# The turn between two transformer layers: an order by hand, weights of the last MLP group split once, first unit's three token tiles in open banks, tables kept in DRAM

## The chip, the cores and the metric

The kernel runs on one core of one Trainium2 chip. The metric is the device time of one launch in microseconds (us), the median of several executions. TensorE is called PE below, VectorE DVE, ScalarE ACT, GpSimd POOL; SP is the engine whose queue issues every DMA of this kernel, strictly in order.

## What is computed

The reference runs two layers over 128 prompt tokens and 512 latent tokens of width 1024, all float32. Cut to what matters here:

```python
def _layer(x, mod, p, lam_init, ctx_kv, rope):
    sh1, sc1, g1, sh2, sc2, g2 = jnp.split(mod, 6, axis=-1)
    h = _rmsnorm(x, p['norm1']) * (1 + sc1) + sh1
    qa, ka, va, qb, kb, vb, uc = jnp.split(h @ p['w_in'], splits, axis=-1)
    qa = _rmsnorm(qa.reshape(b, s, 2, A_HEADS, A_DH), p['qn_a'])      # ka, qb, kb alike
    if rope is not None:
        qa = _apply_rope(qa, cos, sin)                                 # ka, qb, kb alike
    ...
    oa = _diff_attention(qa, ka, va, lam)
    ob = _gqa_attention(qb, kb, vb)
    oc = _pool_mixer(uc, p['w_pool'], p['pool_scale'])
    merged = ga * (oa @ p['w_br_a']) + gb * (ob @ p['w_br_b']) + gc * (oc @ p['w_br_c'])
    x = x + g1 * (merged @ p['w_out'])
    h2 = _rmsnorm(x, p['norm2']) * (1 + sc2) + sh2
    a, g = jnp.split(_dwconv3(h2 @ p['w_up'], p['conv_w'], p['conv_b']), 2, axis=-1)
    x = x + g2 * ((jax.nn.silu(a) * g) @ p['w_down'])
    return x, own_kv
```

Layer 1 starts with the norm of the x that layer 0's last line gives, so nothing of layer 1 can start before x is whole in a token. That turn is the place of the change.

## The kernel before

All 640 tokens stay in SBUF, features on partitions: x is eight blocks of 128 features by 640 tokens. Every matrix product is three matmuls in a rounded 32-bit format (mm3, lines 111 to 114): an operand is split into a high part, written by ACT (line 95), and the rest, written by DVE (line 96). A weight goes through load_w (lines 98 to 106): a DMA into st (three buffers), ACT writes wh, DVE writes wl (five buffers each). A weight is therefore usable one transfer, one ACT instruction and one DVE instruction after its issue.

**The end of a layer.** The MLP's 22 feature blocks are taken in four groups (GROUPS). For the last, blocks 17 to 21, the down projection is made per token chunk, CH_A = (0 to 384), (384 to 640), with a product of five blocks for each of eight outputs n, and the weight of an output is loaded and split again in each chunk: 16 loads of 640 columns (lines 1029 to 1047). After each output DVE adds the product to x (down_add, line 881), ACT squares it, POOL sums the squares over n (DVE the last), and SP stores x to x_dram (line 1043). At the end of a chunk rms1_chunk (line 231) makes the norm: ones times the sum on PE (stat), DVE's ms, POOL's power (rr), one diagonal matrix dg for each 128 tokens on DVE, and ones times dg on PE, which spreads the factor over the partitions (bc). Then modulate (lines 200 to 210) makes the next layer's input: for each feature block k DVE writes ht, ACT the high part hh, DVE the low part hl, in pieces of 128 and 256 tokens.

**The start of a layer.** attention_phase (line 238) first makes the tables of the rotation (cg, sg: lines 247 to 277) on DVE from cos, sin and a few rows of parameters, and the number nlam. Then it works through six units of the input projection. A unit (line 303) has four weights of 768 columns and five token tiles of 128; a tile is eight products of 384 columns in one PSUM bank (mm), which ACT empties into raw (line 361), then squares (366) and sums (368), the rotation (379 to 389) and the transposes (tr) follow. The units are woven with attention tasks of the unit before and with other items ("u" the mixer's input, "g" the gates, "p" the pooling's projection), by the table FILL.

**What sets the order.** No instruction order is written out: the framework's scheduler takes the program and chooses, by a model of its own and the data each instruction needs, the order in which each engine gets it. On the chip each engine works through its list strictly in order, and an instruction that waits holds all behind it.

Of the kernel before, what the change touches and what calls it, by code (L numbers as in the profile page):

```python
# [12 lines left out]
F32 = mybir.dt.float32  # L13
F32R = mybir.dt.float32r
AF = mybir.ActivationFunctionType
ALU = mybir.AluOpType
# [40 lines left out]
def trunk_kernel(ctx: ExitStack, tc: tile.TileContext, a: dict):  # L57
# [34 lines left out]
    x_dram = dram.tile([P, ND, T], F32, name="x_dram")  # L92

# [144 lines left out]
    def attention_phase(l, hh, hl, w0):  # L238
        lam_init = 0.8 - 0.6 * math.exp(-0.3 * l)
        with ExitStack() as st:  # L240
# [5 lines left out]
            rows = ap.tile([P, 8, 64], F32, tag="dup", name="rowv")  # L246
            dma(rows, a["rowv"][l])

            lt = ap.tile([P, 2, 64], F32, tag="sq", name="lt", bufs=4)
            lam2 = small.tile([P, 2], F32, tag="lam2", name="lam2", bufs=1)  # L250
            nlam = small.tile([P, 1], F32, tag="nlam", name="nlam", bufs=1)
            vec.tensor_tensor(out=lt[:, 0], in0=rows[:, 4], in1=rows[:, 5], op=ALU.mult)
            vec.tensor_tensor(out=lt[:, 1], in0=rows[:, 6], in1=rows[:, 7], op=ALU.mult)
            vec.tensor_reduce(out=lam2, in_=lt, axis=AX.X, op=ALU.add)
            act.activation(lam2, lam2, AF.Exp)
            vec.tensor_tensor(out=nlam, in0=lam2[:, 1:2], in1=lam2[:, 0:1], op=ALU.subtract)
            vec.tensor_scalar_add(out=nlam, in0=nlam, scalar1=-lam_init)

            vec.tensor_scalar_mul(out=rows[:, 0:4:2], in0=rows[:, 0:4:2], scalar1=0.125)
            cos = late.tile([P, 4, 64], F32, tag="w", name="cos", bufs=4)  # L260
            sin = late.tile([P, 4, 64], F32, tag="w", name="sin", bufs=4)
            dma(cos, a["cos"])
            dma(sin, a["sin"])
            cgs, sgs = [], []
            for kind in range(2):
                cg = ap.tile([P, 5, 2, 64], F32, tag=f"cg{kind}", name=f"cg{kind}", bufs=1)
                sg = ap.tile([P, 4, 2, 64], F32, tag=f"sg{kind}", name=f"sg{kind}", bufs=1)
                for typ in range(2):
                    g = rows[:, 2 * kind + typ:2 * kind + typ + 1]
                    vec.tensor_copy(cg[:, 0:1, typ], g)  # L270
                    vec.tensor_tensor(out=cg[:, 1:, typ], in0=cos, in1=g.to_broadcast([P, 4, 64]), op=ALU.mult)
                    for h in range(2):
                        hs, ho = slice(32 * h, 32 * h + 32), slice(32 - 32 * h, 64 - 32 * h)
                        vec.tensor_tensor(out=sg[:, :, typ, hs], in0=sin[:, :, hs],
                                          in1=g[:, :, ho].to_broadcast([P, 4, 32]), op=ALU.mult)
                cgs.append(cg)
                sgs.append(sg)
# [25 lines left out]
            def unit(kind, idx, w, out, prefetch):  # L303
# [41 lines left out]
                late_tr = None  # L345
                out.extend((qk, v1, v2))
                for tt in range(5):
                    ts = slice(tt * P, (tt + 1) * P)
                    ps = ps_m.tile([P, 384], F32, tag="mm", name="mm")
                    for k in range(ND):  # L350
                        hi, lo = w[k // 2]
                        ws = slice((k % 2) * 384, (k % 2) * 384 + 384)
                        mm3(ps, hh[:, k, ts], hl[:, k, ts], hi[:, ws], lo[:, ws], k == 0, k == 7)
                        yield 0.49
                    if late_tr is not None:
                        transposes(*late_tr)
                        yield 0.5
# [41 lines left out]
                    late_tr = (dup.rearrange("p h a d -> p h (a d)"), nh, nq, qk, slot)  # L399
                transposes(*late_tr)  # L400
                yield 0.5

# [296 lines left out]
            for i, items in enumerate(FILL):  # L699
                stream.extend([("unit", i)] * (i < len(order)) + items)  # L700
# [16 lines left out]
            def run(i, made=None):  # L717

                kind, n = stream[i]
                w = loaded[i]  # L720
                if kind == "unit":
                    yield from unit(*order[n], w, made, lambda: prefetch(i + 1))
# [9 lines left out]
            for i, items in enumerate(FILL):  # L732
                made = []
                n = len(items)
                if i < len(order):
                    n += 1
                own = chain.from_iterable(run(j, made) for j in range(at, at + n))
# [146 lines left out]


# [85 lines left out]
    sst.close()  # L971
    for l in range(L):
        dst.close()
        xst.close()
        attention_phase(l, hh, hl, w0)
        w0 = None
# [16 lines left out]
        with ExitStack() as ms:  # L993
# [11 lines left out]
            for gi, (f0, f1) in enumerate(GROUPS):  # L1005
# [17 lines left out]
                if l + 1 < L:  # L1023
                    hst = ExitStack()
                    hp = tp("h1p", 1, hst, side="right")
                    hh = hp.tile([P, ND, T], F32R, name="hh")
                    hl = hp.tile([P, ND, T], F32R, name="hl")
                    A1 = scale_cols(l + 1, V_N1, 8, "A1")
                for c, (a0, b0) in enumerate(CH_A):
                    acc = Acc(rp, b0 - a0)  # L1030
                    for n0 in range(0, 8, 2):
                        ps = ps_d.tile("dl")
                        for j in range(2):
                            n = n0 + j
                            hi, lo = load_w(a["w_down"][l, n, :, f0 * P:f1 * P], nf * P)
                            for i in range(nf):
                                ks = slice(i * P, (i + 1) * P)
                                mm3(ps[:, j, :b0 - a0], hi[:, ks], lo[:, ks], fs[i][0][:, a0:b0],
                                    fs[i][1][:, a0:b0], i == 0, i == nf - 1)
                            down_add(l, x, n, ps[:, j], a0, b0)  # L1040
                            if l + 1 < L:
                                acc.add(x[:, n, a0:b0], n == 7)
                                dma(x_dram[:, n, a0:b0], x[:, n, a0:b0])
                            else:
                                dma(a["y"][:, n, a0:b0], x[:, n, a0:b0])
                    if l + 1 < L:
                        rms1_chunk(l + 1, c, rp, x, hh, hl, ps_d, acc, A1)
# [114 lines left out]
```

## Time and profile before

| | |
|---|---|
| median of three runs | 2300.72 us (2298.7 to 2303.47) |
| the profiled execution's own time | 2307.55 us |
| its span in the profile | 2305.3 us |
| mean granted PE clock | 0.988 of full speed |
| busy share of the span: PE, DVE, ACT, POOL | 97%, 68%, 42%, 23% |
| DMA, mean over the span | 112 GB/s |

The profile is one execution. PE's matmuls are pipelined, so their listed durations overlap: the distance from one start to the next is what a matmul costs, and a busy PE can still run at half clock. The shares are means over stages with different limits: what holds between the layers has to be read from the windows there, 1135 to 1230 us.

### The profile page before, as it was taken

To read this page: it belongs to the slowest core of one execution; us is meant where nothing else is said; L and a number is where in the kernel's file an instruction comes from. 1 tells how busy PE (TensorE), PEld (TensorE's weight loads), DVE (VectorE), ACT (ScalarE), POOL (GpSimd) and SP (SyncE) were. 2 spreads that over 40 slices of the span, in tenths; PEclk is the share of its full clock that TensorE was granted. 3 is DMA by queue.
4 is the path that set the end of the run, shared out by engine and by line. 5 is a ranking of instruction groups with operands and counts; after the bars stand their busy time and mean duration, and the time that the engine had idled before them with its cause. 6 is when DMAs were issued, how large, how long until landed. Compare 5 with 4: busy or idle time off the path is not lost. (4 is left out here: it accounts for less than half of the span.)

```text
span 2305.3 us, 37922 instructions
## 1 busy us (share of the span) xinstructions
PE 2225.9 (97%) x14778; PEld 2163.6 (94%) x14778; DVE 1562.8 (68%) x2913; ACT 975.7 (42%) x1728; POOL 528.4 (23%) x651
## 2 busy tenths in 40 slices
PE   8898999999999999999979999999999999999999
PEld 4898989989999999999969989899999999999999
DVE  6877687559567756765587867864895676554555
ACT  4555555432244423333355645653323453242422
POOL 3753443024041000000047533320422200000000
PEclk8999999999999999999999999999999999999999
DMA  7211223367333333432242112224762332322123
GB/s 256 80 57 59 82 66 107 108 244 228 121 121 106 101 104 121 135 102 88 75 128 83 57 49 83 97 89 135 283 210 89 123 110 92 94 65 90 50 84 114
DMA packets 102775, 258.50 MB, mean 112 GB/s; under 512 B 19523, under 2 KB 32579, under 8 KB 102596
## 3 DMA queue, kind: packets, MB, share of 16 engines
q1 hardware_dynamic: 102596, 256.09, 34.1%
q8 instruction: 116, 1.90, 0.3%
q14 instruction: 63, 0.51, 0.1%
HBM read 233.10 MB, written 22.95 MB: 111 GB/s over the span
## 5 line engine op out<-in xcount | busy, mean ns | idle before, releaser
L95 ACT ACTIVATE wh<-st 128x1024 fp32r<-128x1024 f32 (+3 forms) x336 | 314.7, 943 | 297.0 <-PE dn L114 170.8
L113 PE MATMUL up<-h2l,wh 128*128 128x320 f32 x1408 | 435.6, 310 | 2.5 <-DVE h2l L209 2.4
L112 PE MATMUL up<-h2h,wl 128*128 128x320 f32 x1408 | 433.5, 310 | 2.4 <-ACT v L862 1.4
L114 PE MATMUL up<-h2h,wh 128*128 128x320 f32 x1408 | 435.0, 310 | 0.0
L96 DVE TENSOR_TENSOR wl<-st,wh 128x1024 fp32r<-128x1024 f32 (+3 forms) x336 | 375.4, 1120 | 71.7 <-ACT wh L95 71.1
L113 PEld LDWEIGHTS up<-h2l,wh 128*128 128x128 f32 x1408 | 265.2, 189 | 3.6 <-DVE h2l L209 3.6
L112 PEld LDWEIGHTS up<-h2h,wl 128*128 128x128 f32 x1408 | 264.5, 189 | 4.0 <-ACT h2h L208 2.1
L114 PEld LDWEIGHTS up<-h2h,wh 128*128 128x128 f32 x1408 | 265.3, 189 | 0.1
L143 DVE SCALAR_TENSOR_TENSOR junk<-stm,cs 128x1024 bf16<-128x1024 f32 x172 | 223.2, 1298 | 60.1 <-DMA stm<-in_w_mod 57.2
L865 DVE SCALAR_TENSOR_TENSOR v<-u,vecs,v 128x127 f32<-128x127 f32 (+1 forms) x176 | 89.1, 547 | 183.4 <-ACT v L862 183.4
L112 PE MATMUL mm<-wh,hl 128*128 128x384 f32 x480 | 169.5, 353 | 15.0 <-ACT raw L361 10.8
L113 PE MATMUL dn<-al,wh 128*128 128x320 f32 x544 | 168.1, 309 | 0.0
L114 PE MATMUL dn<-ah,wh 128*128 128x320 f32 x544 | 168.1, 309 | 0.0
L112 PE MATMUL dn<-ah,wl 128*128 128x320 f32 x544 | 168.1, 309 | 0.0
L113 PE MATMUL mm<-wl,hh 128*128 128x384 f32 x480 | 163.7, 341 | 2.6 <-DVE wl L96 2.6
L114 PE MATMUL mm<-wh,hh 128*128 128x384 f32 x480 | 163.4, 340 | 0.0
L114 PE MATMUL gp<-hh,wh 128*128 128x320 f32 x480 | 148.6, 310 | 0.0
L112 PE MATMUL gp<-hh,wl 128*128 128x320 f32 x480 | 148.4, 310 | 0.0
L113 PE MATMUL gp<-hl,wh 128*128 128x320 f32 x480 | 148.3, 309 | 0.0
L112 PE MATMUL mmu<-hh,wl 128*128 128x384 f32 (+1 forms) x416 | 134.0, 322 | 4.0 <-ACT up L677 2.0
L114 PE MATMUL mmu<-hh,wh 128*128 128x384 f32 (+1 forms) x416 | 131.0, 315 | 0.0
L113 PE MATMUL mmu<-hl,wh 128*128 128x384 f32 (+1 forms) x416 | 130.4, 314 | 0.0
(226 smaller groups left out, 5444.6 us busy)
## 6 DMA issues: line engine op xcount, KB each, us to landing
stm<-in_w_mod SPq DMA_DIRECT2D x88, 512.0 KB, 4.3
st<-in_w_up SPq DMA_DIRECT2D x88, 512.0 KB, 3.6
st<-in_w_gate SPq DMA_DIRECT2D x48, 512.0 KB, 4.4
st<-in_w_unit SPq DMA_DIRECT2D x48, 384.0 KB, 3.2
st<-in_w_out SPq DMA_DIRECT2D x32, 512.0 KB, 3.6
st<-in_w_down SPq DMA_DIRECT2D x48, 320.0 KB, 3.0
st<-in_w_br SPq DMA_DIRECT2D x24, 512.0 KB, 3.6
st<-in_w_down SPq DMA_DIRECT2D x32, 384.0 KB, 3.2
```

The costliest lines, as they stand in the source:

```text
L95: act.activation(hi, x, AF.Copy)
L96: eng.tensor_tensor(out=lo, in0=x, in1=hi.bitcast(F32), op=ALU.subtract)
L112: pe.matmul(out, sl, mh, start=start, stop=False)
L113: pe.matmul(out, sh, ml, start=False, stop=False)
L114: pe.matmul(out, sh, mh, start=False, stop=stop)
L143: vec.scalar_tensor_tensor(out=junk, in0=st, scalar=1.0, in1=cs[:, j], op0=ALU.mult, op1=ALU.mult, accum_out=col)
L865: vec.scalar_tensor_tensor(out=v[:, s + 1:e], in0=u[:, s:e - 1], scalar=cw[0], in1=v[:, s + 1:e], op0=ALU.mult, op1=ALU.add)
```

## The change

Between layer 0 and layer 1 a new function, turn_over, takes the place of the loop over the two chunks. All of it stands in a block in which every engine keeps the order of the source.

- The weights of the last group are loaded as five tiles of 1024 columns and split once; both chunks use them. They fill all five wh and wl buffers for as long as both chunks run.
- The square of output 0 is written into the sum directly. One diagonal instruction for a whole chunk takes the place of one for each 128 tokens.
- The four weights of layer 1's first unit are loaded within chunk 1, one after the products of each of the outputs 4 to 7.
- The first three token tiles of the first unit are summed in the banks ps_a and ps_b, opened by turn_over. PE's order in that unit is the source's too, and one "u" item moves into it.
- The rotation tables of layer 1 are computed at the end of layer 0's attention (prepare_next), stored to tab_dram and read back by four DMAs in layer 1.

The diff, cut to its core:

```diff
+            def prepare_next():
+                rows = late.tile([P, T], F32, tag="w", name="rowv", bufs=4)...
+                dma(rows, a["rowv"][1])
+                cs2 = rotation()
...
+                for kind, cg, sg in prepare(1, rows, cs2, into):
+                    dma(tab_dram[2 * kind], wide[f"cg{kind}"])
+                    dma(tab_dram[2 * kind + 1][:, :512], wide[f"sg{kind}"][:, :512])
...
+            fill = [FILL[1][:1], FILL[1][1:]] + FILL[2:] if ahead else FILL
...
+                if i == 0 and ahead:
+                    with tc.manual_schedule(engines={mybir.EngineType.PE}):
+                        for _ in run(0, made):
+                            pass
...
+            if l + 1 < L:
+                prepare_next()
             for _ in chain(flush(), *(run(j) for j in range(at, len(stream)))):
...
+    def turn_over(l, x, rp, fs, f0, hh, hl, ps_d, A):
...
+        load(0)
+        load(1)
+        tile_of = lambda c, n: ps_d.pools[(4 * c + n // 2 + 1) % 3].tile([P, 2, 512], F32, tag="d", name="dl")
+        for n in range(8):
+            if n % 2 == 0:
+                ps = tile_of(0, n)
+            products(0, n, ps)
+            if n in (0, 2, 4):
+                load(2 + n // 2)
+            evac(0, n, ps)
+        h0 = None
+        for n in range(8):
+            if n % 2 == 0:
+                ps = tile_of(1, n)
+            products(1, n, ps)
+            if n == 0:
+                last(0)
+            if n == 1:
+                stat(0)
+            if n == 2:
+                diag(0)
+            if n == 3:
+                spread(0)
+            if n >= 4:
+                h0 = h0 or chain(pieces(0, 0, P), pieces(0, P, 384))
+                W0.append(load_w(a["w_unit"][l + 1, 4, n - 4], 768))
+                for _ in range(2):
+                    next(h0)
+            evac(1, n, ps)
+            if n == 1:
+                rstd(0)
...
+        for k in range(ND):
+            unit0(0, k)
+        stat(1)
...
+        for k in range(ND):
+            if k == 3:
+                spread(1)
+            for j in (1, 2):
+                unit0(j, k)
+        for _ in pieces(1, 384, T):
+            pass
+        return W0, ahead
...
+                    with tc.manual_schedule():
+                        w0, ahead = turn_over(l, x, rp, fs, f0, hh, hl, ps_d, A1)
+                    continue
```

Here load(t) is a DMA or more into st, then the split; products(c, n) is the five products of an output; evac is the add to x, the square, POOL's sum and the store to x_dram; pieces is modulate, one feature block a step.

How the lists of the engines stand, at three places. First PE, at the first products of the last group (dl; ah and al are the high and low part of an MLP activation, one pair for each of the five blocks, wl and wh those of the weight). Before, from the fourth product on:

```order
L112 MATMUL dl_12038<-ah_11894,wl_12042 128x384
L113 MATMUL dl_12038<-al_11895,wh_12041 128x384
L114 MATMUL dl_12038<-ah_11894,wh_12041 128x384
L112 MATMUL dl_12094<-ah_11178,wl_12098 128x384
L113 MATMUL dl_12094<-al_11179,wh_12097 128x384
L114 MATMUL dl_12094<-ah_11178,wh_12097 128x384
```

Now, from the fourth product on:

```order
L114 MATMUL dl_12096<-ah_11935,wl_12085 128x384
L115 MATMUL dl_12096<-al_11936,wh_12084 128x384
L116 MATMUL dl_12096<-ah_11935,wh_12084 128x384
L114 MATMUL dl_12096<-ah_12067,wl_12085 128x384
L115 MATMUL dl_12096<-al_12068,wh_12084 128x384
L116 MATMUL dl_12096<-ah_12067,wh_12084 128x384
```

Before, the fifth product of the first output stands later and another output's first product comes in its place; now it follows the fourth.

Second SP's queue around the loads of the first unit (st<-in_w_unit), among the stores of x (384 columns in chunk 0, 256 in chunk 1). Before:

```order
L1043 DMA x_dram<-x 128x384
L102 DMA st<-in_w_unit 128x768
L1043 DMA x_dram<-x 128x256 x2
L102 DMA st<-in_w_unit 128x768 x2
L1043 DMA x_dram<-x 128x256
L102 DMA st<-in_w_unit 128x768
L1043 DMA x_dram<-x 128x256
```

Now:

```order
L990 DMA x_dram<-x 128x384 x4
L990 DMA x_dram<-x 128x256 x4
L104 DMA st<-in_w_unit 128x768
L990 DMA x_dram<-x 128x256
L104 DMA st<-in_w_unit 128x768
L990 DMA x_dram<-x 128x256
L104 DMA st<-in_w_unit 128x768
L990 DMA x_dram<-x 128x256
L104 DMA st<-in_w_unit 128x768
L104 DMA st<-in_w_u 128x1024
```

The first unit load has moved from behind the last store of chunk 0 to behind the fourth of chunk 1, and each of the next stands behind one store more. DVE's list at the same place, before:

```order
L881 SCALAR_TENSOR_TENSOR x<-dl,mod_88,x 128x256 x2
L96 TENSOR_TENSOR wl<-st,wh 128x640 x2
L881 SCALAR_TENSOR_TENSOR x<-dl,mod_88,x 128x256
L187 TENSOR_SCALAR ms<-stat 128x3
L168 COPY acc<-sq 128x256
L96 TENSOR_TENSOR wl<-st,wh 128x768
L197 TENSOR_SCALAR dg<-ident,rr 128x128 x2
L881 SCALAR_TENSOR_TENSOR x<-dl,mod_88,x 128x256
L96 TENSOR_TENSOR wl<-st,wh 128x768
```

Now:

```order
L942 SCALAR_TENSOR_TENSOR x<-dl,mod_88,x 128x256 x2
L98 TENSOR_TENSOR wl<-st,wh 128x768
L1030 SCALAR_TENSOR_TENSOR ht<-x,A_12077,bc_12375 128x128 x2
L1025 SCALAR_TENSOR_TENSOR hl<-ht,mod_91,hh 128x128
L942 SCALAR_TENSOR_TENSOR x<-dl,mod_88,x 128x256
L98 TENSOR_TENSOR wl<-st,wh 128x768
L1030 SCALAR_TENSOR_TENSOR ht<-x,A_12077,bc_12375 128x128
L1025 SCALAR_TENSOR_TENSOR hl<-ht,mod_91,hh 128x128
L1030 SCALAR_TENSOR_TENSOR ht<-x,A_12077,bc_12375 128x128
L1025 SCALAR_TENSOR_TENSOR hl<-ht,mod_91,hh 128x128
L942 SCALAR_TENSOR_TENSOR x<-dl,mod_88,x 128x256
L98 TENSOR_TENSOR wl<-st,wh 128x768
```

Each x add of outputs 4 to 7 stands directly behind the split of a unit weight and the ht and hl of the first token tile.

Third SP's queue at the end of layer 0's attention, where the merge reads its first operands (so<-o_dram). Before:

```order
L526 DMA o_dram<-o 128x640
L650 DMA g_dram<-z 128x640
L102 DMA st<-in_w_br 128x1024 x2
L759 DMA so<-o_dram 128x640 x4
L102 DMA st<-in_w_gate 128x1024
```

Now:

```order
L574 DMA o_dram<-o 128x640
L303 DMA rowv<-in_rowv 128x512
L283 DMA cos<-in_cos 128x256
L312 DMA tab_dram<-cg_5144 128x640
L698 DMA g_dram<-z 128x640
L104 DMA st<-in_w_br 128x1024
L284 DMA sin<-in_sin 128x256
L104 DMA st<-in_w_br 128x1024
L313 DMA tab_dram<-sg_5145 128x512
L312 DMA tab_dram<-cg_5156 128x640
L313 DMA tab_dram<-sg_5157 128x512
L820 DMA so<-o_dram 128x640 x3
```

The loads of the parameters and the four stores of the tables now stand ahead of the first operands.

## Rows read from the trace of the kernel before

**Rows 1.** Windows between the layers: stretch; length, busy per engine, PE clock, DMA share, GB/s

```profile
1170.00:1180.00 10.00, 6.07 (x38) 4.67 (x37) 9.73 (x25) 6.28 (x15) 5.20 (x5) 1.00 0.68 208
1180.00:1190.00 10.00, 7.18 (x35) 5.21 (x35) 9.49 (x35) 5.90 (x13) 5.31 (x10) 1.00 0.21 72
1190.00:1200.00 10.00, 8.53 (x45) 7.19 (x44) 9.78 (x25) 6.36 (x16) 2.67 (x5) 1.00 0.07 16
1200.00:1210.00 10.00, 5.94 (x35) 5.62 (x35) 9.37 (x30) 2.84 (x12) 6.69 (x11) 0.95 0.10 30
1210.00:1220.00 10.00, 9.22 (x48) 8.87 (x47) 9.94 (x21) 5.10 (x8) 8.17 (x12) 0.87 0.44 123
```

**Rows 2.** Timeline of PE, 1135 to 1215: start, duration, instruction, [idle before <-releaser]

```profile
1135.48 0.34 PE L112 MATMUL dl<-ah,wl 128*128 128x384 f32 x1
1135.65 0.34 PE L113 MATMUL dl<-al,wh 128*128 128x384 f32 x1
...
1208.60 0.45 PE L112 MATMUL mm<-wh,hl 128*128 128x384 f32 x1 [4.06 <-ACT raw L361]
...
1209.34 0.52 PE L112 MATMUL mm<-wh,hl 128*128 128x384 f32 x1
1209.66 0.52 PE L113 MATMUL mm<-wl,hh 128*128 128x384 f32 x1
...
1214.84 0.34 PE L114 MATMUL mm<-wh,hh 128*128 128x384 f32 x1
```

**Rows 3.** Timeline of DVE, 1141 to 1206

```profile
1141.52 0.83 DVE L96 TENSOR_TENSOR al<-v,ah 128x640 fp32r<-128x640 f32 x1 [0.80 <-ACT ah L95]
...
1166.94 0.96 DVE L96 TENSOR_TENSOR wl<-st,wh 128x768 fp32r<-128x768 f32 x1 [1.56 <-ACT wh L95]
...
1177.59 0.94 DVE L96 TENSOR_TENSOR wl<-st,wh 128x768 fp32r<-128x768 f32 x1
...
1184.13 0.47 DVE L206 SCALAR_TENSOR_TENSOR ht<-x,A,bc 128x256 f32<-128x256 f32 x1
...
1198.17 0.87 DVE L206 SCALAR_TENSOR_TENSOR ht<-x,A,bc 128x256 f32<-128x256 f32 x2
...
1200.54 0.47 DVE L209 SCALAR_TENSOR_TENSOR hl<-ht,mod,hh 128x256 fp32r<-128x256 f32 x1
...
1201.34 1.41 DVE L271 TENSOR_TENSOR cg<-cos,rowv 128x256 f32<-128x256 f32 x4
1202.98 3.05 DVE L274 TENSOR_TENSOR sg<-sin,rowv 128x128 f32<-128x128 f32 x8 [0.23 <-DMA sin<-in_sin]
```

**Rows 4.** Timeline of SP's queue, 1162: the first unit load

```profile
1162.02 0.33 SPq L102 DMA_DIRECT2D st<-in_w_unit  x1
```

**Rows 5.** Unit weight loads, issue to landing: all 48, then 1155 to 1185's eight

```profile
DMA to landing us min/median/max: 2.8/3.2/8.0
...
DMA to landing us min/median/max: 3.2/4.0/5.5
```

**Rows 6.** Groups by line and shape, 1135 to 1215: busy us, mean ns | idle before

```profile
L171 POOL TENSOR_TENSOR acc<-acc,sq 128x256 f32<-128x256 f32 x6 | 6.7, 1110 | 3.8 <-ACT sq L165 3.7
...
L95 ACT ACTIVATE wh<-st 128x768 fp32r<-128x768 f32 x8 | 6.7, 843 | 8.2 <-DMA st<-in_w_unit 5.1 <-PE mm L114 2.9 <-PE dl L114 0.2
...
L361 ACT ACTIVATE raw<-mm 128x384 f32<-128x384 f32 x4 | 2.0, 489 | 0.3 <-PE mm L114 0.3
...
L118 POOL TENSOR_TENSOR rr<-ms,mhalf 128x3 f32<-128x3 f32 x1 | 0.9, 860 | 7.1 <-DVE ms L187 7.1
```

**Rows 7.** Timeline at layer 0's merge, 447 to 467: SP's queue, then DVE

```profile
447.65 8.28 SPq L759 DMA_DIRECT2D so<-o_dram  x4
...
458.40 1.73 DVE L96 TENSOR_TENSOR ol<-so,oh 128x640 fp32r<-128x640 f32 x2
...
466.05 0.82 DVE L809 TENSOR_TENSOR m<-bp,gt 128x640 f32<-128x640 f32 x1 [0.97 <-PE bp L114]
```

**Rows 8.** A window in layer 1's attention, columns as in Rows 1

```profile
1330.00:1340.00 10.00, 7.20 (x34) 6.54 (x33) 9.73 (x21) 3.50 (x12) 1.87 (x5) 0.60 0.17 52
```

More of the change, by code (lines that the diff above doesn't have):

```diff
@@ L92, in trunk_kernel @@
     x_dram = dram.tile([P, ND, T], F32, name="x_dram")
+    tab_dram = dram.tile([4, P, 640], F32, name="tab_dram")
+    nlams = [const.tile([P, 1], F32, name=f"nlam{l}") for l in range(L)]
     def split(x, hi, lo, eng=vec):
@@ L236, in rms1_chunk, with prepare, attention_phase @@
         modulate(rp, x, bc, A, B, a0, b0, hh[:, :, a0:b0], hl[:, :, a0:b0])
-    def attention_phase(l, hh, hl, w0):
+    def prepare(l, rows, cs2, into):
+        lam_init = 0.8 - 0.6 * math.exp(-0.3 * l)
+        lt = into("lt")[:, :128].rearrange("p (a d) -> p a d", a=2)
+        lam2 = small.tile([P, 2], F32, tag="lam2", name="lam2", bufs=1)
+        vec.tensor_tensor(out=lt[:, 0], in0=rows[:, 4], in1=rows[:, 5], op=ALU.mult)
+        vec.tensor_tensor(out=lt[:, 1], in0=rows[:, 6], in1=rows[:, 7], op=ALU.mult)
+        vec.tensor_reduce(out=lam2, in_=lt, axis=AX.X, op=ALU.add)
+        act.activation(lam2, lam2, AF.Exp)
+        vec.tensor_tensor(out=nlams[l], in0=lam2[:, 1:2], in1=lam2[:, 0:1], op=ALU.subtract)
+        vec.tensor_scalar_add(out=nlams[l], in0=nlams[l], scalar1=-lam_init)
+        vec.tensor_scalar_mul(out=rows[:, 0:4:2], in0=rows[:, 0:4:2], scalar1=0.125)
+        cos, sin = cs2
+        for kind in range(2):
+            cg = into(f"cg{kind}").rearrange("p (t a d) -> p t a d", t=5, a=2)
+            sg = into(f"sg{kind}")[:, :512].rearrange("p (t a d) -> p t a d", t=4, a=2)
+            for typ in range(2):
+                g = rows[:, 2 * kind + typ:2 * kind + typ + 1]
+                vec.tensor_copy(cg[:, 0:1, typ], g)
+                vec.tensor_tensor(out=cg[:, 1:, typ], in0=cos, in1=g.to_broadcast([P, 4, 64]), op=ALU.mult)
+                for h in range(2):
+                    hs, ho = slice(32 * h, 32 * h + 32), slice(32 - 32 * h, 64 - 32 * h)
+                    vec.tensor_tensor(out=sg[:, :, typ, hs], in0=sin[:, :, hs],
+                                      in1=g[:, :, ho].to_broadcast([P, 4, 32]), op=ALU.mult)
+            yield kind, cg, sg
+    def attention_phase(l, hh, hl, w0, ahead=None):
         lam_init = 0.8 - 0.6 * math.exp(-0.3 * l)
@@ L244, in attention_phase @@
             ps_m = tp("ps_m", 1, st, space=PSUM)
[L246 to L277, printed above, removed]
+            tabs = {}
@@ new lines, in own, with rotation @@
+            def own(name):
+                tabs[name] = ap.tile([P, 640 if name[0] == "c" else 512], F32, tag=name, name=name, bufs=1)
+                return tabs[name]
+            def rotation():
+                cos = late.tile([P, 4, 64], F32, tag="w", name="cos", bufs=4)
+                sin = late.tile([P, 4, 64], F32, tag="w", name="sin", bufs=4)
+                dma(cos, a["cos"])
+                dma(sin, a["sin"])
+                return cos, sin
+            if l == 0:
+                rows = ap.tile([P, 8, 64], F32, tag="dup", name="rowv")
+                dma(rows, a["rowv"][0])
+                for _ in prepare(0, rows, rotation(),
+                                 lambda n: own(n) if n != "lt" else ap.tile([P, 640], F32, tag="dup", name="lt")):
+                    pass
+            else:
+                for k, n in enumerate(("cg0", "sg0", "cg1", "sg1")):
+                    dma(own(n), tab_dram[k] if n[0] == "c" else tab_dram[k][:, :512])
@@ L721, in run @@
                 if kind == "unit":
-                    yield from unit(*order[n], w, made, lambda: prefetch(i + 1))
+                    if i == 0 and ahead:
+                        yield from unit(*order[n], w, made, lambda: prefetch(i + 1), ahead, run(1))
+                    else:
+                        yield from unit(*order[n], w, made, lambda: prefetch(i + 1))
                     return
@@ L971, in trunk_kernel @@
     sst.close()
+    ahead = None
     for l in range(L):
```

158 lines of the change are left out of this document (133 added, 25 removed).

## The prediction

> **What bounds the kernel now.** I read the page first (PE is busy for nearly the whole span, so a change can only pay where PE waits), then the ten-microsecond windows between the layers, then the timelines of PE, DVE and SP there. The windows [rows 1] show the place: from 1170 to 1220 PE is busy 6 to 9 of every 10 us, while DVE is at 9.4 to 9.9. So at the end of the turn from layer 0 to layer 1 DVE sets the pace. All times T below count from the first product of the last w_down group, 1135.48; the last of unit 0's 40 products (of three matmuls each) starts at 1214.84, T 79.4 [rows 2]. That stretch holds 40 products of 384 columns, 40 of 256 and unit 0's 40 of 384: at the full-speed spacing of 0.17 us a matmul, by columns 0.52, 0.35 and 0.52 us a product, 56 us, and some 3 for the small matmuls. About 20 us are lost, 4.06 of them in one wait at 1208.60, after which the matmuls come 0.32 us apart instead of 0.17 for 3 us [rows 2]. Behind this wait stand the rotation tables, 1.41 + 3.05 us of DVE at 1201 to 1206 [rows 3]. These 20 us are what the change can win; it can also make them more.
>
> **The change part by part.** *Less DVE work.* 16 splits of 640 columns (0.83 us each, as al, which has that size) become 5 of 1024, by columns from the 0.96 us of a 768 split [rows 3] 1.28 each: 13.3 - 6.4 = 6.9 us less. Most of it lies before 1170, where DVE is not the bound, so I count it nothing; the cover is the chain below. The tables, 4.5 us and small instructions that I put at 1.5, leave the end of the turn, where DVE is the bound: -6 us, and the 4.06 us wait goes with them. That is inside the sum that follows, because I rebuild the whole DVE list rather than subtract from before.
>
> *PE in source order.* Before ran the first four products of three outputs ahead, so that the fifth, which needs the last MLP activation, came late. After has the fifth product of output 0 in fifth place. It needs al, which ends at 1141.52 + 0.83 = T 6.9 [rows 3]; one split less stands ahead of it (-0.8), so T 6.05. Four products end at T 2.1: PE stands 3.9 us. Nothing else is let past it.
>
> *Chunk 0's weights.* SP issues in order. The fourth load stands behind the x stores of outputs 0 and 1, the fifth behind those of 2 and 3, and each store waits for its x add. Each of these loads then costs a trip: the issue 0.35, the landing 3.2, ACT's high half about 1.1, DVE's low half 1.28. From output 1's end (T about 10) the fourth is ready at 16.2, when PE wants it at 16.3. From output 3's end (T about 17.3) the fifth is ready at 23.9, and PE wants it at 20.4: it stands 3.5 us. Chunk 0 ends at 20.8 + 3.9 + 3.5 = T 28.1.
>
> *The step that decides: four trips in a row in chunk 1.* After asks for unit 0's four weights one at a time, between outputs 4, 5, 6 and 7. On SP each load stands behind the x store of the output before. On DVE each x add stands behind the split of the weight before. So the load waits for the store, the store for the add, the add for the split, and the split for the load. Before had six or more x adds and stores clear ahead, and its first unit load went out at 1162.02, T 26.5 [rows 4], and its fourth weight's split [rows 3] ended at 1177.59 + 0.94, T 43. In after the chain begins with the x add of output 3. PE's outputs 0 and 1 end at 28.1 + 3.6 = 31.7; x, square and POOL's sum (about 0.45, 0.45 and 1.1) come before the 0.86 of the reciprocal root [rows 6], then the diagonal (about 0.55) and two x adds (0.87, as two ht [rows 3]): with small waits T 36.2. One trip is the issue 0.33 [rows 4] + 0.05, the landing, 0.84 for the high half [rows 6] and 0.96 for the low [rows 3]: 2.2 us plus the landing. For the landing I take 3.2 us, the page's median of 48 such loads, since these go out alone; in the turn of before, under heavy traffic, the median is 4.0 [rows 5]. Between trips lie 3 or 4 of ht and hl (0.3 each) and an x add (0.47): 4.7 us for the three gaps. Sum: 4 x 5.4 + 4.7 = 26.3, so the fourth weight is ready at T 62.5 instead of 43.
>
> *Then the DVE list.* Up to the last hl of tile 0: five of ht/hl, the split of the next weight (1.28), x and the last sum: 3.5, T 66.0. Tiles 1 and 2: 16 of ht/hl at the 0.40 step (0.87 - 0.47 of the row at 1198.17 [rows 3]) and 0.9 of small ones: T 73.3. Tiles 3 and 4: 16 more, 6.4, with unit 0's own work between. For that I take what before has between its first and last wide ht/hl: 1184.13 to 1201.0 are 16.9 us, its 32 at 0.40 take 12.8, so 4.1 [rows 3]. T 83.8. PE then needs one product (0.5) for tile 3, waits for ACT to empty the single bank (0.49 [rows 6]) and does tile 4's eight products (4.2): the last begins near T 89, **9.5 us later than before**. The tables gone and the wait at 1208 gone are in this number. The three open banks give tiles 0 to 2 PE work early, but hl paces them in both kernels, so I count that at nothing; its cover is the DVE list, and without it it would be worth the few waits of about 1 us on raw.
>
> *Layer 0 pays for the tables.* They are computed near the end of layer 0's attention. DVE has slack there, but SP does not: the four stores to tab_dram stand ahead of the so loads, and the tables need cos and sin, whose space comes free when PE has used the last pair's. Before issues the first so loads at 447.65 [rows 7]. Six us of DVE work and a landing later is about 455. The third and fourth ol end at 460.1 and the products that they enter end before the m of 466.05 [rows 7], so about 4 to 5 us of 7 are covered: I take +1.5, between 0 (the stores go early) and +3 (7 less 4).
>
> *Layer 1's attention* gets its order shifted: one in_u item moves into unit 0. PE loses most at 1330 to 1340 (busy 7.2, clock 0.60, DVE 9.73 [rows 8]), and a DVE list that ends elsewhere can win or lose there. I take 0, bounds -4 and +4. The four table loads (1.2 MB) stand on SP in a quiet stretch, and their cover is the ht/hl work: nothing.
>
> **Sum:** 9.5 + 1.5 + 0 = **+11.0 us**. On the profiled run's own 2307.55 that is 2318.5. That run lies 6.8 above the median of 2300.72, and I carry the difference to the median: **2311.7**.
>
> **A rule weighed.** The unit loads of before land in 2.8 us at best, 3.2 at the median and 4.0 where the queues are full [rows 5]. The Trainium skill, DMA: Bandwidth & Descriptors, "Anatomy of one DMA", puts a fixed part of about 2.0 us on each DMA, whatever its size, and 2.0 + bytes/436e3 for the whole (measured on the other issuing path): an estimate of 2.9 us for this load. By it four trips would be 1.2 us shorter and the sum +9.8. It speaks against the change, as a fixed part is paid once for each trip that waits for the one before.
>
> **The rivals.**
> *Faster (chance 0.20).* The trips are hidden, because the SP or DVE order lets the unit loads leave before the x adds that I put ahead of them, or the adds come early. Then DVE's list bounds as before, but 6 us shorter, and the half-clock stretch (9 matmuls x 0.15 = 1.3) goes too; with 1 us given back in layer 0 that is -6 to -8: **2293.5**. For: DVE is the bound in [rows 1], and it loses work. Against: the order of the two queues as it stands. It decides once a trip with its gap costs under some 4.2 us instead of 7 (11 us over four); the landing alone is most of that.
> *About the same (0.13).* Short landings (2.8: -1.6 over four trips and -0.8 in chunk 0), layer 0 free (-1.5) and 4 us won back at 1320 to 1340, with 2 us of my DVE list too long: +1, **2302**.
> *Slower still (0.15).* The clock. PE falls to half speed after the wait before 1209 [rows 2], and in after it is nearly idle from T 38 to 62. If half speed lasts through the last ten products, 30 matmuls at 0.32 instead of 0.17 add 4.5; landings of 4.0 add 3.2, layer 0 another 1.5: +20, **2321**. For: several gaps longer than 4 us. Against: in 1170 to 1180 PE is busy for 6.07 of 10 and its clock stays at 1.00 [rows 1], so gaps shorter than these leave it alone, and DVE paces tiles 3 and 4 anyway. The Trainium skill, TensorE: Matmul & The Clock Gate, Part 1, has the slow clock as the default that activity lifts, which goes this way; the row at 1170 shows that a partly busy engine is spared here.
> *As forecast (0.52).* Four trips, clock mostly full.
>
> **How the numbers follow.** The likeliest case gives 2311.7, its own range 2304 to 2320: landing 2.8 to 4.0 (-2.4 to +3.2), layer 0 (-1.5 to +1.5), layer 1 (-4 to +4), not all at once. The range that should hold 8 in 10 goes down to 2295, which leaves out most of the faster case's lower part, some 0.12, and up to 2325, which leaves out about 0.06. A time within 0.2% of before (2296.1 to 2305.3) is about what a measurement can't tell from no change. Faster than that takes the faster case: 0.20. The middle takes the same case and a little of the forecast's low end: 0.15. Slower: 0.65.
>
> **What would show it.** Right: in the trace of after the four unit loads issue about 7 us apart, each within 0.5 us of an x add; DVE idle before each of their splits for 3 us or more, PE under half busy from T 38 to 62; a PE wait of about 4 us near T 2 on al; the last of the 40 products near T 89; the tables gone from there. In layer 0 the first so load near 455. Wrong: unit loads issued close together or before T 35, the fourth split before T 50, or DVE still at 9.5 of 10 there; then the faster case holds. If the turn ends at T 89 but the total does not move, layer 1's attention has given it back.

## The result and the profile after

The changed kernel takes **2338.6 us** (median of four runs, 2338.0 to 2344.0), against 2301.0 for the kernel before: a ratio of **1.0168 [1.015, 1.0187]**, 37.6 us slower. The forecast was slower by 11.0 us (2311.7, range 2295 to 2325): the direction held, the size did not.

The profiled run of after is the 2343.99 one. The first lines of its page, with the granted clock in 40 slices:

```profile
span 2342.2 us, 37850 instructions
PE 2235.5 (95%) x14772; PEld 2177.6 (93%) x14772; DVE 1554.1 (66%) x2897; ACT 972.5 (42%) x1717; POOL 527.8 (23%) x651
PEclk8999999999999999999888999999999999999999
```

Its span is 36.9 us longer than that of before, and nearly all of it comes in the turn between the layers. The first product of the last w_down group starts at 1135.86 (T 0 of after; 1135.48 in before [rows 2]), a difference of 0.4; it tells nothing by itself, since T 0 lies from 1129.5 to 1134.4 in the experiments below, which have the layer 0 of after. The last of unit 0's 40 products starts at 1248.35, T 112.5. In before it starts at 1213.94, T 78.5: the matmul of 1214.84 [rows 2], T 79.4, is the third of that product, not the first.

```profile
1213.94 0.34 PE L112 MATMUL mm<-wh,hl 128*128 128x384 f32 x1
```

So the turn up to there is 34.0 us longer, and 2.5 more follow behind it. The windows of after, with the columns of [rows 1]:

```profile
1140.00:1150.00 10.00, 6.11 (x32) 5.47 (x32) 1.75 (x5) 1.05 (x2) 1.01 (x1) 1.00 0.28 92
1150.00:1160.00 10.00, 6.89 (x30) 6.86 (x30) 2.62 (x5) 2.10 (x3) 1.77 (x2) 0.66 0.11 40
1160.00:1170.00 10.00, 4.76 (x16) 4.47 (x15) 1.88 (x3) 1.58 (x2) 1.25 (x2) 0.68 0.23 73
1190.00:1200.00 10.00, 4.90 (x23) 4.81 (x23) 2.22 (x5) 2.45 (x5) 0.73 (x1) 0.72 0.28 89
1200.00:1210.00 10.00, 2.10 (x12) 1.90 (x11) 4.88 (x13) 3.58 (x8) 0.72 (x1) 0.67 0.16 52
1230.00:1240.00 10.00, 6.61 (x33) 5.12 (x31) 9.82 (x27) 6.29 (x15) 7.54 (x13) 0.94 0.08 18
1250.00:1260.00 10.00, 6.66 (x27) 6.52 (x27) 8.61 (x18) 5.03 (x15) 5.30 (x5) 0.66 0.56 184
```

In [rows 1] DVE was at 9.4 to 9.9 and set the pace. In after it is at 2 to 5 until 1210, and PE is low too: no engine is the bound there, each waits for another. Who waits for what, PE's waits of after from 1135 to 1262 (us in total, times, the longest), and under them the one row of before for the same wait in the same stretch:

```profile
PE dl L114 <- DVE x L942: 20.1, 7, 5.8
PE dl L114 <- DVE sqe L318: 7.9, 1, 7.9
PE mm L114 <- DVE hl L1025: 6.5, 6, 1.9
PE tr L329 <- DVE qk L333: 3.3, 1, 3.3
```

```profile
PE dl L112 <- DVE x L881: 0.3, 1, 0.3
```

The first row is a wait that the prediction did not have at all. The second row is the same wait once more: in DVE's list the small memset sqe stands directly behind the x add of output 6 in chunk 1, and the profile names the later of the two.

```profile
1209.06 0.48 DVE L942 SCALAR_TENSOR_TENSOR x<-dl,mod,x 128x256 f32<-128x256 f32 x1
1209.49 0.06 DVE L318 MEMSET sqe<- 128x5 f32 x1
```

So there are eight such waits, 28.0 us in all, and not seven with 20.1, as the expectations below still have it: 12.8 in chunk 0, 2.3 in the first half of chunk 1, and 5.1 + 7.9 before outputs 5 and 7, within the trips. PE's timeline shows its cause (a group's start, its time, and in brackets the idle time before it):

```profile
1139.46 0.44 PE L114 MATMUL dl<-ah,wl 128*128 128x384 f32 x1 [1.22 <-ACT ah L97]
1140.32 0.44 PE L115 MATMUL dl<-al,wh 128*128 128x384 f32 x1 [0.42 <-DVE al L98]
1141.78 0.44 PE L114 MATMUL dl<-ah,wl 128*128 128x384 f32 x1 [0.84 <-DVE x L942]
1153.11 0.69 PE L114 MATMUL dl<-ah,wl 128*128 128x384 f32 x1 [5.84 <-DVE x L942]
1165.53 0.69 PE L114 MATMUL dl<-ah,wl 128*128 128x384 f32 x1 [5.24 <-DVE x L942]
1174.14 0.44 PE L114 MATMUL dl<-ah,wl 128*128 128x384 f32 x1 [0.84 <-DVE x L942]
1195.19 0.58 PE L114 MATMUL dl<-ah,wl 128*128 128x256 f32 x1 [5.10 <-DVE x L942]
1209.59 0.58 PE L114 MATMUL dl<-ah,wl 128*128 128x256 f32 x1 [7.90 <-DVE sqe L318]
1221.71 0.69 PE L114 MATMUL mm<-wh,hl 128*128 128x384 f32 x1 [0.85 <-DVE hl L1025]
1240.62 0.69 PE L114 MATMUL mm<-wh,hl 128*128 128x384 f32 x1 [1.10 <-DVE hl L1025]
1248.35 0.34 PE L114 MATMUL mm<-wh,hl 128*128 128x384 f32 x1
1253.76 1.33 PE L329 MATMUL tr<-ident,dup 128*128 128x128 f32 x5 [3.34 <-DVE qk L333]
```

Outputs n and n+1 (n even) lie in the two banks of one PSUM tile. The first product of the odd output waits until DVE has added the even one to x, though it writes the other bank. In source order this wait stands in front of PE for every pair. That it comes from the two banks being one tile is read off the names and the order: no run gives each output a tile of its own. DVE at the second of them:

```profile
1144.71 0.74 DVE L942 SCALAR_TENSOR_TENSOR x<-dl,mod,x 128x128 f32<-128x128 f32 x2 [2.98 <-PE dl L116]
1151.18 1.23 DVE L98 TENSOR_TENSOR wl<-st,wh 128x1024 fp32r<-128x1024 f32 x1 [5.73 <-ACT wh L97]
1152.32 0.74 DVE L942 SCALAR_TENSOR_TENSOR x<-dl,mod,x 128x128 f32<-128x128 f32 x2
1157.73 0.74 DVE L942 SCALAR_TENSOR_TENSOR x<-dl,mod,x 128x128 f32<-128x128 f32 x2 [4.67 <-PE dl L116]
1163.59 1.23 DVE L98 TENSOR_TENSOR wl<-st,wh 128x1024 fp32r<-128x1024 f32 x1 [5.12 <-ACT wh L97]
```

The add of output 2, at 1152.32, is ready long before, but in DVE's list it stands behind the split of the fourth w_down tile, and DVE stands 5.73 us there. The split waits for a load, and SP's queue shows when that went out:

```profile
1145.90 1.35 SPq L959 DMA_DIRECT2D st<-in_w_down  x3
1158.92 0.87 SPq L959 DMA_DIRECT2D st<-in_w_down  x2
1188.63 0.38 SPq L104 DMA_DIRECT2D st<-in_w_unit  x1
1195.58 0.39 SPq L104 DMA_DIRECT2D st<-in_w_unit  x1
1203.26 0.38 SPq L104 DMA_DIRECT2D st<-in_w_unit  x1
1209.99 0.37 SPq L104 DMA_DIRECT2D st<-in_w_unit  x1
```

At 1145.90, 0.45 us after the x add of output 1 (1144.71 + 0.74), behind whose store it stands. So the trip that the prediction put between SP, ACT and DVE runs through PE as well: store, load, split, x add, then the matmuls of the next output, whose own add the next store waits for. The four unit loads, 6.95, 7.68 and 6.73 us apart, are the serial trips of the forecast (7 us apart).

### The profile page after: what moved, and what is told of

It is laid out like the page before. It is cut to its first block, busy times and chain, and to the rows that moved or that the text cites. A ratio compares the mean times of both kernels' runs of the same rounds, so it can differ in the third digit from the quotient of the medians.

```text
span 2342.2 us, 37850 instructions
## 1 busy us (share of the span) xinstructions
PE 2235.5 (95%) x14772; PEld 2177.6 (93%) x14772; DVE 1554.1 (66%) x2897; ACT 972.5 (42%) x1717; POOL 527.8 (23%) x651
## 5 line engine op out<-in xcount | busy, mean ns | idle before, releaser
L98 DVE TENSOR_TENSOR wl<-st,wh 128x1024 fp32r<-128x1024 f32 (+3 forms) x325 | 367.4, 1133 | 108.8 <-ACT wh L97 107.8
L97 ACT ACTIVATE wh<-st 128x1024 fp32r<-128x1024 f32 (+3 forms) x325 | 308.5, 955 | 303.3 <-PE dn L116 170.9
```

Of the source, the lines that this page charges most:

```text
L97: act.activation(hi, x, AF.Copy)
L98: eng.tensor_tensor(out=lo, in0=x, in1=hi.bitcast(F32), op=ALU.subtract)
```

## The experiments

Theory A: the 37.6 us come from the written order, as two losses: PE's wait on the add of the even output (the shared tile), and loads queued behind stores. Rival B: the open banks, the single split or the tables cost the time themselves. Rival C: one engine's list alone is at fault, and freeing it repairs the turn. The experiments take the losses away one at a time, then both, then the whole order, then parts of the change and of the order.

**The wait on the pair, alone.** Both outputs of a pair get their products before either is emptied, in both chunks:

```diff
-            products(0, n, ps)
+                products(0, n, ps)
+                products(0, n + 1, ps)
...
```

> Edit: in both chunks the products of the outputs n and n+1, which share one two-bank PSUM tile, are issued one behind the other before either is added to x. Theory A (PE waits for the x add of the even output before it may begin the odd one, 20.1 us of PE idle time in the turn, and this delayed the start of the four weight trips by 16 us): the seven waits of PE dl on DVE x fall from 20.1 to under 8 us, the first unit load goes out about 15 us earlier after the first product (T 38 instead of T 52.8), the four trips stay at 7 us each, total about 2323 us (2318 to 2328). Rival B (the trips alone set the time and the waits on x lie beside them): under 4 us gained, 2335 to 2339.

Measured: 2324.3 (1.0102 [1.0086, 1.0117]), 14.3 us less than after. The wait on x is gone from PE's list, and the unit loads still go out 7.4, 7.1 and 6.8 us apart. PE's two largest waits and the first two of the loads:

```profile
PE mm L114 <- DVE hl L1025: 17.4, 8, 5.8
PE dl L114 <- DVE wl L98: 5.9, 2, 4.7
```

```profile
1175.51 0.41 SPq L104 DMA_DIRECT2D st<-in_w_unit  x1
1182.89 0.38 SPq L104 DMA_DIRECT2D st<-in_w_unit  x1
```

The first load leaves at 1175.51 and not 1188.63; counted from the first product of this run (1133.87) that is T 41.6 and not T 52.8, 11 us earlier where I expected 15. The pair wait moved the start of the trips, not the trips.

**The trips, alone.** Only the DMAs of the four unit weights move up; the splits stay where they were:

```diff
+            if n >= 6:
+                fetch(n - 6)
...
-                W0.append(load_w(a["w_unit"][l + 1, 4, n - 4], 768))
+                W0.append(halves(n - 4))
+                if n == 4:
+                    fetch(3)
```

(The third goes out at output 0 of chunk 1.)

> Edit: only the DMAs of the four unit weights move earlier (two among the last stores of chunk 0, one at the first output of chunk 1, one at output 4); their splits stay where they were on ACT and DVE. Theory A (each of the four trips waits for a landing, about 4.3 us of DVE idle time each): DVE's idle time before the four splits falls from 4.3 to 5.2 us each to under 1, from the x add of output 3 to the fourth split 9 to 12 us instead of 26.9, total about 2322 us (2317 to 2327). Rival B (the waits of PE on x set the time and the trips lie beside them): under 4 us gained.

Measured: 2328.0 (1.0118 [1.0098, 1.0137]), 10.6 us less, not 16, and outside the range. From the x add of output 3 to the fourth split it is 13.4 us, not 9 to 12. PE's eight waits on x are 20.2 us and not 28.0: those of chunk 0 stay (12.5 against 12.8), and the last two of chunk 1 fall from 5.1 + 7.9 to 1.9 + 3.6, for these had held the trips within them. DVE still stands at each split, for 1.28 us:

```profile
PE dl L114 <- DVE x L942: 20.2, 8, 5.6
```

```profile
1185.61 0.96 DVE L98 TENSOR_TENSOR wl<-st,wh 128x768 fp32r<-128x768 f32 x1 [1.28 <-ACT wh L97]
1189.32 0.96 DVE L98 TENSOR_TENSOR wl<-st,wh 128x768 fp32r<-128x768 f32 x1 [1.28 <-ACT wh L97]
```

The splits are 3.71 us apart instead of about 7. What is left of a trip needs no load: ACT's high half stands behind the square of the output before, which waits for an x add behind the split of the weight before. I had taken the load away and forgotten that ACT's list is a ring too.

**Both.**

> Edit: the two edits before together. Theory A (two chains in a row, each paid in full): the gains add up, 15 + 16 us, total about 2307 us (2300 to 2312), with some more if PE's clock no longer falls. Rival B (one of the two hides the other): no better than the better one of the two by more than 4 us.

Measured: 2310.5 (1.0043 [1.003, 1.0055]). 28.1 us come back, about the 14.3 + 10.6 of the two alone, so the two losses add. DVE before the last two w_down splits shows what is left of the slow part:

```profile
1145.13 1.22 DVE L98 TENSOR_TENSOR wl<-st,wh 128x1024 fp32r<-128x1024 f32 x1 [5.52 <-ACT wh L97]
1153.38 1.23 DVE L98 TENSOR_TENSOR wl<-st,wh 128x1024 fp32r<-128x1024 f32 x1 [5.72 <-ACT wh L97]
```

**The w_down loads as well.** The DMAs of the fourth and fifth tile go out before the first x store, on top of both edits:

```diff
+            if n == 0:
+                get(3)
+                get(4)
```

> Edit: e3_both, and the DMAs of the fourth and fifth w_down tile go out with the third, ahead of the first x store; their splits stay where they were. Theory A (in chunk 0 too a load behind a store costs a trip: DVE was idle 5.5 and 5.7 us before these two splits and PE 0.9 + 3.8 us): DVE's wait before both splits goes to zero, chunk 0 ends 4 to 5 us earlier after the first product, total about 2306 us (2302 to 2308). Rival B (PE catches up later, where DVE paces): under 2 us, 2309 to 2312.

Measured: 2299.1 (0.9994 [0.9983, 1.0005]), 11.4 us less than with both and not 4.5. The two splits wait 1.54 and 1.60 us now. In the traces of the two the turn is 7.1 us shorter (the last of unit 0's products starts at T 75.1 and not 82.2): the 0.9 + 3.8 us that PE waited for the splits, and some 1.5 in ten matmuls that came 0.32 us apart behind the second wait. I had counted the first part alone; where the rest of the 11.4 comes from stays open.

**A better order by hand.** In addition the fifth products last in the first pair, and the unit splits at outputs 2, 3, 5 and 6:

```diff
+                products(0, n, ps, range(4))
+                products(0, n + 1, ps, range(4))
+                products(0, n, ps, range(4, 5))
+                products(0, n + 1, ps, range(4, 5))
...
+            if n in (2, 3, 5, 6):
+                W0.append(halves(len(W0)))
```

> Edit: e5_early, and the first two outputs leave their fifth products to the end of the pair, and the four unit splits stand at outputs 2, 3, 5 and 6 instead of 4 to 7 (their DMAs earlier to match). Theory A (the order is all that is wrong, so one that has no load, no split and no late activation in front of an x add comes near the scheduler's): the wait on al goes (1.6 us), the 1.28 us wait before each unit split goes (5 us), total about 2299 us (2293 to 2304). Rival C (an order written out has a cost of its own that these repairs do not reach): 2304 us or more.

Measured: 2297.2 (0.998 [0.997, 0.999]). The wait on al is gone; three of the four waits of 1.28 us before the unit splits stayed. The interval overlaps that of the version above, so the gain of this step is not settled. A good order by hand has thus no cost left that shows: 2297.2 is 0.2% faster than before, and the interval overlaps that of the free order below.

**The whole order given back.** The block that fixes it is taken off; PE in unit 0 stays in source order:

```diff
-                    with tc.manual_schedule():
-                        w0, ahead = turn_over(l, x, rp, fs, f0, hh, hl, ps_d, A1)
+                    w0, ahead = turn_over(l, x, rp, fs, f0, hh, hl, ps_d, A1)
```

> Edit: the change as it is, but the order of the turn between the layers is left to the scheduler as before; only PE's order in the first unit stays written out. Theory A (the order of the four queues is what costs, not the single split, the banks or the tables): about 2300 us or below (2290 to 2306), PE waits on x under 3 us in the turn. Rival C (the weights that hold all five buffers through both chunks cost, whatever the order): over 2320 us.

Measured: **2294.5** (0.9974 [0.9962, 0.9986]): 44.1 us less than after, with the same work, tiles and banks. The first unit load leaves at 1135.13, T 4.2, and the other three from 1160.01 to 1168.33, near the 1162.02 of [rows 4]; PE's wait on x is almost nothing:

```profile
PE dl L114 <- DVE x L942: 0.6, 1, 0.6
```

```profile
1135.13 0.33 SPq L104 DMA_DIRECT2D st<-in_w_unit  x1
1160.01 0.33 SPq L104 DMA_DIRECT2D st<-in_w_unit  x1
```

Theory A holds: the whole loss is the order, and under another order the change is some 6 us faster than before.

**The parts.** First, the kernel above without the open banks (unit 0's sums in its own bank again):

```diff
-        mms = [pool_.tile([P, 2, 512], F32, tag="d", name="mm0") for pool_ in (ps_a, ps_b)]
...
-        return W0, ahead
+        return W0, ()
```

> Edit: e4_free (the scheduler's order) without the three open banks: the first three token tiles of unit 0 are made by the unit itself, in its one bank, and the u item goes back to its old place. Theory A (hl paces tiles 0 to 2, so the banks are worth little): within 3 us of e4_free, 2292 to 2298. Rival D (the banks carry what e4_free gains over the kernel before): 2299 to 2304.

Measured: 2294.0 (0.9965 [0.9951, 0.9978]). The banks are worth nothing that can be told. In this run DVE paces there, as it did in [rows 1]:

```profile
1190.00:1200.00 10.00, 7.94 (x52) 7.28 (x51) 9.88 (x26) 4.41 (x10) 6.67 (x12) 1.00 0.01 2
1200.00:1210.00 10.00, 8.35 (x51) 8.13 (x50) 9.08 (x21) 7.95 (x20) 7.15 (x11) 1.00 0.35 104
```

Second, the kernel before with only the tables moved:

```diff
+            if l + 1 < L:
+                prepare_next()
```

> Edit: the kernel before with the tables part of the change alone (computed at the end of layer 0's attention, through tab_dram); turn, splits and banks as before. Theory A (the tables' 6 us stand on DVE where DVE paces, and the 4.06 us wait of PE stands behind them): about 2295 us (2292 to 2298), the wait before 1209 gone, layer 0 unchanged within 1 us. Rival E (the time is given back, by the later first operands of layer 0's merge or in the attention that follows): 2299 to 2304.

Measured: 2296.2 (0.9973 [0.9963, 0.9983]). The 4.06 us wait of [rows 2] is gone; the longest one left behind 1200 is this:

```profile
1207.26 0.74 PE L329 MATMUL tr<-ident,dup 128*128 128x128 f32 x5 [1.56 <-DVE dup L430]
```

The tables carry most of the change's gain, if not all of it: 5.3 us by the medians, and by the ratios (0.9973 here, 0.9974 and 0.9965 for the two kernels above) it can't be told from the whole. What the single split and the rest of the change add, some 2 us by the medians, is not settled, as the intervals overlap. Rival B falls: with the order free, tables, banks and single split together cost nothing.

**One engine's list at a time.** Four kernels keep the written order on some engines and leave the rest to the scheduler, by one line each (here the first):

```diff
-                    with tc.manual_schedule():
+                    with tc.manual_schedule(engines={mybir.EngineType.SP, mybir.EngineType.DVE,
+                                                     mybir.EngineType.Activation, mybir.EngineType.Pool}):
```

> Edit: the change as it is, but in the turn only SP, DVE, ACT and POOL keep the written order; PE's is the scheduler's, which runs even outputs of other tiles ahead of the odd ones. Theory A (PE's waits on x are one of two chains): the waits of PE dl on DVE x fall from 20 to under 5 us, the four unit loads still go out 7 us apart, total as e1_pairs or a little below, 2321 us (2315 to 2327). Rival B (PE's order costs nothing by itself): 2335 to 2339.

> Edit: the change as it is, but SP's order is the scheduler's; it sends three unit loads and the last two w_down tiles ahead of the stores of chunk 0. PE, DVE, ACT and POOL keep the written order. Theory A: as e2_fetch (2328) less what the loads of chunk 0 cost behind stores (11 us between e3_both and e5_early): 2318 us (2312 to 2326), PE's waits on x near 10 us or more. Rival B (SP's order costs nothing by itself): 2335 to 2339.

> Edit: the change as it is, but only PE keeps the written order in the turn. Theory A (a wait of PE on the x add of the even output costs about 0.9 us where no split and no load stands ahead of that add, and 16 us arose because they did): eight such waits, 7 to 8 us, and 1.6 us for the late activation: e4_free + 9 = 2303 us (2299 to 2308). Rival F (PE's order alone costs the 16 us): 2309 us or more.

> Edit: the change as it is, but DVE's order is the scheduler's; SP still sends each unit load behind the store of the output before. Theory A (the trips are in a row only because the x adds stand behind the splits on DVE): the unit loads go out under 4 us apart, total about 2309 us (2303 to 2316). Rival G (SP's order alone makes the trips): they stay 7 us apart, 2325 us or more.

| kept by hand | PE waits on x, us | median, us | ratio to before |
|---|---|---|---|
| all five (after) | 28.0 | 2338.6 | 1.0168 [1.015, 1.0187] |
| all but PE | 3.8 | 2333.6 | 1.0141 [1.0124, 1.0158] |
| all but SP | 12.8 | 2314.8 | 1.0058 [1.0041, 1.0074] |
| all but DVE | 6.6 | 2311.6 | 1.0042 [1.0026, 1.0058] |
| PE alone | 6.9 | 2305.8 | 1.0017 [1.0008, 1.0027] |
| none (unit 0's PE only) | 0.6 | 2294.5 | 0.9974 [0.9962, 0.9986] |

The first of the four missed (I expected 2321). With PE's list free its two costliest waits are:

```profile
PE mm L114 <- DVE hl L1025: 19.9, 8, 7.2
PE dl L114 <- DVE wl L98: 12.9, 2, 7.5
```

The pair waits fell as expected, but PE's new list runs into a w_down tile whose load stands behind stores in SP's fixed queue, and stands there. The other three came inside their ranges. PE by hand with all else free waits 6.9 us in 8 times, 0.9 each: that is the bare price of the shared tile (the kernel is 11.3 us above the free order, so PE's order costs some more than these waits). With the stores and splits in the way it becomes 28.0, and what hangs on it more. With DVE free the unit loads close up to 2.4, 4.3 and 1.0 us apart (I had said under 4): only the first split still stands ahead of an add that a load waits for, and the adds of outputs 5 and 6 come 0.9 us apart behind it (1181.65 and 1182.56). Rival C falls for PE, SP and DVE: each of these four kernels has at least one list given back, and only the one that keeps PE's alone comes within 0.2% of before. The lists of ACT and POOL were not freed alone.

## Why the prediction was right or wrong

- **The four trips: right.** Forecast 26.3 us from the x add of output 3 to the fourth split; measured 1188.18 to 1215.10, 26.9. DVE stands 4.52 and 4.59 us before the first and the last of the splits, PE is busy 4.9 and 2.1 of 10 there. The five unit loads of after from 1188 to 1211 land in 3.2 us at the median, as in [rows 5]. By the fixed part that the Trainium skill, DMA: Bandwidth & Descriptors, "Anatomy of one DMA", gives a DMA, an estimate for the four trips is 25.1; the trace is nearer to 3.2 us a landing than to that estimate's 2.9. The sign "PE under half busy from T 38 to 62" came later, from T 54 to 74, because the trips began later.
- **"Chunk 0's weights" and the start of the trips: this is the step that failed.** It had the fourth tile ready at T 16.2 (measured 1152.41, T 16.6) and PE arriving just then. But PE was not there: it stood 5.84 us for an add behind that very split. It gave PE one stall of 3.5 us for the fifth tile; PE stood 12.8 us in four waits on x (0.84, 5.84, 5.24, 0.84), and its clock fell. Chunk 0 ended at T 41.2, not 28.1: 20.8 of products, 1.6 on ah and al, 12.8 on x, and about 6 that are left, some 4 of them in 26 matmuls that came 0.32 us apart or more and not 0.17, at a clock of 0.66 and 0.68 from 1150 to 1170. In chunk 1 two more waits on x (0.72, 1.54) stand ahead of the trips. The x add of output 3 in chunk 1 ended at T 52.3 instead of 36.2: **16 us** of the 26 that the sum lacked. The step's own arithmetic was off as well: 20 products of 0.52 and 3.9 put output 3's end at 14.3, not at "about 17.3", and with 14.3 its stall for the fifth tile would have been 0.5 and not 3.5.
- Why it was missed: before's own trace has the wait, once, 0.3 us. The scheduler ran even outputs of other tiles in between, as the first order list of the change shows (dl_12038 then dl_12094, two tiles). I read PE's new list for the data that each product needs, and not for the space that it writes.
- **The wait on al: mis-sized.** 3.9 forecast, 1.22 + 0.42 measured; al ends at T 4.4: the one split that I counted has left from ahead of it, and the DVE work that leads to it begins at 1135.84, T 0.0, where in before it began at 1137.19, T 1.7. It only offset the rest.
- **The DVE list behind the trips: mis-sized.** From the fourth split to the last of the 40 products 26.5 us forecast, 33.3 measured (1215.10 to 1248.35): +6.8. From the rows of ht and hl of 256 columns, some 1.4 of it is unit 0's own DVE work (5.5 and not 4.1), 1.4 a DVE wait on the diagonal's product, and some 1.5 lies behind the last hl (it ends at 1241.7), where PE's matmuls come 0.32 us apart until 1245.6 (granted clock 0.72 from 1240 to 1250). The other 2.5 I have not split further.
- **Behind unit 0: missing.** PE waits 3.34 us for DVE at 1253.76 and runs at 0.66 in 1250 to 1260; from the last of unit 0's products to the end of the span after takes 2.5 us more than before. I had this place at 0, with bounds of 4.
- **Layer 0: wrong, by little.** +1.5 forecast, none that shows. The so loads left 4.7 us later (452.37 against 447.65 [rows 7]), but the m that they feed starts at 465.93, before at 466.05: the cover I had counted as 4 to 5 us held it all.
- **The start of the comparison: read 0.9 late.** The last product of before starts at T 78.5 and not 79.4, so the forecast T 89 stood for 10.4 us and not 9.5.
- **The rival "slower still"** (a clock that stays low) named the right second effect: some 100 matmuls of 384 or 256 columns came at half the rate between 1130 and 1262, some 14 in before. Over full-rate spacing that is about 13 us of PE's time against 2. I take it for no cause of its own, since it stands behind waits and most of it goes with them (some 23 such matmuls, 3 us, with the order free); no run changes the clock alone. The "faster" rival's price, 2293.5, is near what the freed order measures (2294.5): the gain that I saw was there, and the order hid it. The rival also had the half-clock stretch gone, and that did not come: the clock with the order free is 0.68 and 0.84 in 1190 to 1200 and 1200 to 1210.

Sum by the steps, against the forecast's +11: 16.1 (pair waits and clock in front of the trips) + 0.6 (trips) + 6.8 (list behind) + 2.5 (behind unit 0) + 0.9 (the start read late) - 1.5 (layer 0) + 0.4 (T 0) is 25.8, and 36.8 in all; the span grew by 36.9.

## What to carry to other kernels

When an order that a scheduler made is fixed by hand, write down for each engine what the instruction in front waits for, and count the space it writes as well as the data it reads: two banks that belong to one tile are one resource here, and a wait of 0.3 us that reordering hid became 28. In queues that keep their order, put loads ahead of stores, and a split never ahead of the add that something else waits for; otherwise the waits close into a ring and each round of it costs a whole trip, landing included (about 7 us here). One list mended alone moved the wait to another engine; here it took three edits by hand, to PE's list and to SP's, or giving the order back, to return to before.

The best kernel of these runs is the changed one with the order left to the scheduler, 2294.0 to 2294.5 us with or without the open banks: 0.3% faster than before.

## What the runs showed of the hardware

TensorE's clock fell at waits. In the PE rows of after, the first product behind a wait of 5.84 or 5.24 us takes 0.69 us and behind one of 0.84 or 1.22 us 0.44; at 256 columns it is 0.58 behind 5.10 and 7.90 us. The windows agree: 0.66 granted in 1150 to 1160, a mix of the two levels (1.2 and 2.4 GHz), where PE is busy 6.89 of 10. In [rows 1] it was busy 6.07 from 1170 to 1180 and stayed at 1.00, so the busy share of a stretch alone doesn't tell which one is slowed. Nor does the last wait alone: at 1221.71 and 1240.62 a product behind waits of only 0.85 and 1.10 us takes 0.69 us; a wait of 1.63 stands before the first of them, waits of 1.92, 0.50 and 0.48 before the second. In before the first product behind the wait of 4.06 us still takes 0.45, and those from 1209.34 on take 0.52 [rows 2], so there the clock fell after PE had begun again. The Trainium skill, TensorE: Matmul & The Clock Gate, Part 1, has the slow clock as the default that activity lifts; these rows fit that.
